# Two-layer hybrid decoder in FP32: operands of the down projection made ahead, their buffers and PSUM banks changed, modulation columns three per step

## The chip, the cores and the metric

The kernel runs on one core of a Trainium2 chip, as one program. The metric is the device time of one execution in microseconds (us), lower is better. Five engines work side by side, each in its own order, and wait for each other by semaphores: PE (TensorE, matmuls; the profile shows its weight loads apart as PEld), DVE (VectorE), ACT (ScalarE), POOL (GpSimd) and SP (SyncE, which here only issues loads and stores). Matmuls write PSUM, which is divided into 8 banks of 512 FP32 columns.

## The reference

The input x is 512 tokens of 1024 channels. Each of two layers has a mixer (an S5 state space part and differential attention) and a SwiGLU feed-forward part, with shift, scale and gate vectors made from a conditioning vector c by one matrix product per layer ("modulation"). The change is in the feed-forward part, which computes

```
m    = silu(c) @ mod_w[l] + mod_b[l]        # 6 x 1024 numbers per layer
h2   = x * (1 + scale2) + shift2
a    = silu(h2 @ w_gate[l]) * (h2 @ w_up[l])   # 512 x 2816
y    = a @ w_down[l]                           # 512 x 1024
x    = layer_norm(alpha * x + gate2 * y)
```

All is FP32.

## The kernel before

FP32 accuracy is had from three matmuls in a faster format: every operand is split into a high part, rounded by ACT, and a low part, the difference, made by DVE; `mm3` issues high x high, high x low and low x high. One use of 128 x 128 weights for 512 tokens is 3 matmuls.

**Weights.** `wunit` loads 512 KB (`wraw`, 2 buffers, issued by SP), lets ACT make `whi` and DVE `wlo` (5 buffers each). They run ahead of PE as far as buffers are free.

**Gate and up.** The 2816 hidden channels are 22 blocks of 128, `fi` = 0 to 21. A step `fi` has two weight units and 48 matmuls into a pair of PSUM banks (`gps`). `swiglu` then has ACT make `sg` and DVE `aT`, and hangs two pieces of background work behind it: `build_bg`, a step of building the S5 tables of the next layer (DVE, POOL, ACT, some PE: `kps` products and `qps` transposes), and `mods_bg`, which computes the modulation columns that were loaded in the step before (a load of 512 KB into `mraw`, a multiplication with a sum on DVE) and issues the loads of the next ones. In layer 0 these are 48 columns: 8 of this layer, whose last are the gate vector `G`, and 40 of the next. Their buffers are the five of tag "C", which `gb`, `G` and `ah` use too.

**Down.** The output is made in two halves of 512 channels, n = 0 and 1, each for four blocks of 128 tokens, t = 0 to 3, into four PSUM banks (`dps`). The loop goes over 11 pairs `fp` of hidden blocks: a weight unit, then for both blocks the operand `ah`, its high part by ACT and its low part by DVE, then 12 matmuls for each block (3 for each t). The last pairs (`TAIL`: 2 in layer 0, 4 in layer 1) are held back and run token block by token block, and after each block `resid_half` multiplies by the gate vector (`rtmp`, DVE), adds to x and takes statistics. In n=1 of layer 0 `norm` and the transposes `htp` for the next layer follow. `gate_tile` writes the gate columns to DRAM (`gd`) and loads them back spread over all partitions (`G`), after the last held `ah`, by a copy on POOL that serves as the order.

PSUM has two banks `acc`, one `s5`, one `po` and two tiles `patt` of two banks each. What waits for a tile waits for all of it: if one half of a pair is read by DVE, a matmul into the other half that stands behind it waits for the read.

What each engine runs, and in what order, follows from the order in the code and a scheduler that keeps it free of waits as far as it can see; `queued` ties background work behind what stands before it.

Of the kernel before, what the change touches and what calls it, by code (L numbers as in the profile page):

```python
# [10 lines left out]
F32R = mybir.dt.float32r  # L11
# [51 lines left out]
def trunk_kernel(tc, xT, x, c, pos, modw, modb, wst, s5a, s5bc, s5d, glub, lamv, subw, lng, lnr, out):  # L63
# [3 lines left out]
    with ExitStack() as es:  # L67
# [257 lines left out]
        def new_hT(name, tag="hT"):  # L325
            hi = [u4(tag, [P, 2, T], F32R, name=f"{name}h{i}") for i in range(4)]
            lo = [u4(tag, [P, 2, T], F32R, name=f"{name}l{i}") for i in range(4)]
            return hi, lo
# [565 lines left out]
        def mods_bg(cols, n, ring, skip=()):  # L894

            with queued(marks(), skip):
                while pend:
                    pend.pop(0)()
                for _ in range(n):
                    if cols:  # L900
                        pend.append(mod_load(*cols.pop(0), ring))
# [33 lines left out]
        for l in range(L):  # L935
# [258 lines left out]
            def swiglu(fi, pgu):  # L1194
                sg = t2([P, T], name="sg")
                nc.scalar.activation(sg, pgu[:, 0], AF.Silu)
                tt(aT[fi // 2][:, fi % 2], sg, pgu[:, 1], ALU.mult)
                if fi > 1:
                    build_bg(builds)
                mods_bg(cols, 2, "C")  # L1200
                if 2 <= fi < 6:
                    with queued(marks()):
                        affine(xt[fi - 2], gb)
# [5 lines left out]
                    gate_up(fi, pgus[fi], w2s[fi], sl)  # L1209
            for fi in range(2):  # L1210
                swiglu(fi, pgus[fi])
            for fi in range(2, NF):
                pgu = patt("gps")
                gate_up(fi, pgu, [wunit(wb + 26 + 2 * fi + i) for i in range(2)], slice(0, T))
                swiglu(fi, pgu)
            sts = [sm([P, 2, 6], "bnst", 5) for _ in range(NT)]
            hTn = new_hT("hTn") if l + 1 < L else None
            TAIL = 2 if l + 1 < L else 4
            for n in range(2):
                if n == 0:  # L1220
                    pss = [patt("dps") for _ in range(2)]
                    pss = [pss[t // 2][:, t % 2] for t in range(NT)]
                else:
                    pss = [acc("dps"), acc("dps"), ppo("dps"), ps5("dps")]

                def dn(fi, w, f2, t, ah):
                    mm3(pss[t], (ah[:, 0, tok(t)], ah[:, 1, tok(t)]), rows(w, f2), fi == 0, fi == NF - 1)

                held = []
                for fp in range(NF // 2):  # L1230
                    w = wunit(wb + 70 + 11 * n + fp)
                    for f2 in range(2):
                        fi = 2 * fp + f2
                        last = l + 1 == L and fp >= NF // 2 - TAIL
                        ah = u4("hT" if last else "C", [P, 2, T], F32R, name="ah")
                        cp(ah[:, 0], aT[fp][:, f2])
                        tt(ah[:, 1], aT[fp][:, f2], f(ah[:, 0]), ALU.subtract)
                        if fp < NF // 2 - TAIL:
                            for t in range(NT):
                                dn(fi, w, f2, t, ah)  # L1240
                        else:
                            held.append((fi, w, f2, ah))
                    if n == 0:
                        build_bg(builds)
                        mods_bg(cols, 1, None)
                if n == 1 and l + 1 < L:
                    gb = load_gb(2 * l + 1, f(held[-1][3][:, 0, 0:1]))
                if n == 0:
                    assert not cols and not builds and not pend
                    G2 = gate_tile(l, 1, f(held[-1][3][:, 0, 0:1]))  # L1250
                    abn = mod_ab(l + 1, 0, 2 * l + 1) if l + 1 < L else None
                for t in range(NT):
                    for fi, w, f2, ah in held:
                        dn(fi, w, f2, t, ah)
# [107 lines left out]
```

## Time and profile before

| | |
|---|---|
| runs | 1279.36, 1279.63, 1282.85 us; median 1279.63 |
| profiled execution | 1279.54 us, span of its instructions 1277.8 us |
| PE busy | 1190.9 us, 93% of the span |
| DVE busy | 841.6 us, 66% |
| ACT busy | 478.9 us, 37% |
| POOL busy | 206.4 us, 16% |
| chain that ended last | PE 68%, DVE 18%, DMA 4%, POOL 3%, issue 3%, ACT 3% |
| mean load, `wraw` / `mraw` | 3.7 / 4.8 us to landing (median), 512 KB each |

The shares are means over the whole program. In the timeline a row gives start, length, engine, line, operation, output and inputs, and in brackets the idle time of the engine before it and what ended it. PEclk is TensorE's granted clock as a part of full speed.

### The profile page before, as it was taken

The page shows a single profiled execution, that of the slowest core. Times are in us where ns is not written, and L with a number is a line of the kernel's source. Part 1 is how long each engine was busy: PE and PEld are TensorE (multiplying, and loading weights), DVE is VectorE, ACT ScalarE, POOL GpSimd, SP SyncE. Part 2 cuts the span into 40 slices and gives each one's busy share as a digit, 9 for nine tenths or more (in the row PEclk, how much of TensorE's full clock was granted, in tenths as well). Part 3 has the DMA queues.
Part 4 walks back from the last instruction along what each step waited for, and adds up shares of the span by engine and source line. Part 5 has one row for each costly group of instructions (what it writes and reads, how often), then busy time and mean ns, then how long its engine had stood idle before and what let it go on. Part 6 is the DMA issues. An engine that isn't in the chain of part 4 may idle for free.

```text
span 1277.8 us, 17430 instructions
## 1 busy us (share of the span) xinstructions
PE 1190.9 (93%) x6608; PEld 992.1 (78%) x6608; DVE 841.6 (66%) x1537; ACT 478.9 (37%) x846; POOL 206.4 (16%) x286
## 2 busy tenths in 40 slices
PE   4768888999999999989899999999999999999997
PEld 3557777688888888867687798878888888888885
DVE  6679999866687576698647557785666222235556
ACT  3413446527322222243346245661733222234330
POOL 8943320001002121132001131100000000000001
PEclk8887999999999999999899999999999999999999
DMA  9654236534665666744333554423463333333241
GB/s 357 226 153 143 65 82 226 158 107 152 195 221 186 226 200 193 252 141 146 117 99 101 186 168 107 131 83 99 151 196 103 98 96 100 99 99 115 66 133 66
DMA packets 66868, 186.57 MB, mean 146 GB/s; under 512 B 7936, under 2 KB 21536, under 8 KB 66784
## 3 DMA queue, kind: packets, MB, share of 16 engines
q1 hardware_dynamic: 62352, 174.88, 43.4%
q0 software_dynamic: 2848, 8.70, 2.1%
q10 hardware_dynamic: 1584, 1.88, 0.5%
q8 instruction: 52, 0.85, 0.3%
q14 instruction: 32, 0.26, 0.1%
HBM read 171.85 MB, written 11.49 MB: 143 GB/s over the span
## 4 chain that ended last, share of the span: by engine, by line
PE 68%; DVE 18%; DMA 4%; POOL 3%; issue 3%; ACT 3%; SPq 0%; DVEq 0%; POOLq 0%; ACTq 0%
PE gps L116 37%; PE dps L116 14%; PE ops L116 4%; PE vps L116 3%; DVE mraw L110 3%; PE ups L116 2%; PE qkps L116 2%; DVE wlo L104 2%; DVE stmp L104 1%; POOL s5tmp L104 1%; DMA mraw<-in_modw 1%; DMA wraw<-in_wst 1%; DVE Gt L104 1%; PE yps L116 1%; PE glups L116 1%
## 5 line engine op out<-in xcount | busy, mean ns | idle before, releaser
L104 DVE TENSOR_TENSOR wlo<-wraw,whi 128x1024 fp32r<-128x1024 f32 x180 | 225.3, 1254 | 266.3 <-ACT whi L113 264.4
L113 ACT ACTIVATE whi<-wraw 128x1024 fp32r<-128x1024 f32 x184 | 194.2, 1058 | 376.6 <-PE gps L116 273.0
L116 PE MATMUL gps<-hT2h,whi 128*128 128x512 f32 (+1 forms) x768 | 286.4, 373 | 0.2
L116 PE MATMUL gps<-hT2l,whi 128*128 128x512 f32 (+1 forms) x768 | 285.7, 372 | 0.0
L116 PE MATMUL gps<-hT2h,wlo 128*128 128x512 f32 (+1 forms) x768 | 285.3, 372 | 0.0
L116 PE MATMUL dps<-whi,ah 128*128 128x512 f32 x704 | 223.7, 397 | 8.2 <-DVE rtmp L104 4.5
L116 PEld LDWEIGHTS gps<-hT2h,whi 128*128 128x128 f32 x768 | 144.6, 188 | 25.8 <-DVE rtmp L104 0.6
L116 PEld LDWEIGHTS dps<-whi,ah 128*128 128x128 f32 x704 | 133.9, 190 | 39.5 <-DVE rtmp L104 6.0
L116 PEld LDWEIGHTS gps<-hT2h,wlo 128*128 128x128 f32 x768 | 144.7, 188 | 25.1
L116 PEld LDWEIGHTS gps<-hT2l,whi 128*128 128x128 f32 x768 | 144.7, 188 | 24.9
L116 PE MATMUL dps<-wlo,ah 128*128 128x512 f32 x352 | 138.5, 393 | 0.0
L110 DVE SCALAR_TENSOR_TENSOR mraw<-mraw,scb 128x1024 f32<-128x1024 f32 x96 | 122.0, 1299 | 1.8 <-DMA mraw<-in_modw 1.6
L113 ACT ACTIVATE ah<-aT 128x512 fp32r<-128x512 f32 x88 | 53.8, 627 | 115.5 <-PE dps L116 93.2
L104 DVE TENSOR_TENSOR ah<-aT,ah 128x512 fp32r<-128x512 f32 x88 | 61.1, 706 | 40.0 <-ACT ah L113 39.6
L116 PEld LDWEIGHTS dps<-wlo,ah 128*128 128x128 f32 x352 | 67.2, 191 | 13.6
L116 PE MATMUL qkps<-whi,hTh 128*128 128x256 f32 x128 | 39.7, 312 | 7.3 <-ACT whi L113 6.5
L116 PE MATMUL ops<-whi,am 128*128 128x512 f32 x128 | 43.4, 398 | 0.0
L116 PE MATMUL qkps<-wlo,hTh 128*128 128x256 f32 x128 | 40.0, 313 | 0.5 <-DVE wlo L104 0.5
L104 POOL TENSOR_TENSOR rs<-rs,mhalf 128x1 f32<-128x1 f32 x16 | 10.8, 676 | 176.8 <-DVE rs L101 176.8
L116 PE MATMUL qkps<-whi,hTl 128*128 128x256 f32 x128 | 39.1, 306 | 0.0
L751 ACT ACTIVATE e<-sps,nm 128x128 f32<-128x128 f32 (+3 forms) x64 | 33.1, 525 | 14.9 <-DVE nm L749 12.8
L116 PE MATMUL qkps<-whi,hTnh 128*128 128x256 f32 x128 | 37.4, 292 | 0.0
(290 smaller groups left out, 1939.4 us busy)
## 6 DMA issues: line engine op xcount, KB each, us to landing
wraw<-in_wst SPq DMA_DIRECT2D x184, 512.0 KB, 3.7
mraw<-in_modw SPq DMA_DIRECT2D x96, 512.0 KB, 4.8
M<-kd SPq DMA_DIRECT2D x64, 64.0 KB, 3.6
gb<-in_lnr SPq DMA_DIRECT2D x8, 512.0 KB, 4.1
xT<-in_xT SPq DMA_DIRECT2D x8, 256.0 KB, 7.1
u<-us SPq DMA_DIRECT2D x32, 64.0 KB, 2.5
csl<-sC SPq DMA_DIRECT2D x8, 256.0 KB, 2.8
x<-in_x SPq DMA_DIRECT2D x4, 512.0 KB, 4.1
```

Of the source, the lines that this page charges most:

```text
L104: (eng or nc.vector).tensor_tensor(out, a, b, op=op)
L110: nc.vector.scalar_tensor_tensor(out, a, s, b, op0=ALU.mult, op1=ALU.mult, accum_out=acc_out)
L113: nc.scalar.activation(out, in_, AF.Copy, scale=scale)
L116: nc.tensor.matmul(ps, a, b, start=start, stop=stop)
L751: nc.scalar.activation(e[:, m, :n], ps[:, m, :n], AF.Exp, bias=nm[:, m : m + 1], accum_out=ss[:, i, m : m + 1])
```

## The change

Four things are changed, and both layers run the same code.

1. Modulation columns: two per step for `fi` under 3, then three.
2. The weights and `ah` of pair (n, fp) = (0, 0) are made ahead of gate and up step 21, those of (0, 1) behind its matmuls, and those of (1, 0) ahead of the token blocks of n = 0 (`operands`, kept in `ready`).
3. In layer 0 the `ah` of n = 0 use the eight "hT" buffers instead of "C", but for the ones made ahead; `hTn`, which also needs "hT", is allocated only after the loop of n = 1.
4. PSUM banks: n = 0 uses `acc`, `acc` and one pair (t = 2, 3); n = 1 uses a pair (t = 0, 1), `po` and `s5`. Before, n = 0 used two pairs, and n = 1 `acc`, `acc`, `po`, `s5`.

```diff
-                mods_bg(cols, 2, "C")
+                mods_bg(cols, 2 if fi < 3 else 3, "C")
...
+            ready = {}
+
+            def operands(n, fp, tag):
+
+                w, ahs = wunit(wb + 70 + 11 * n + fp), []
+                for f2 in range(2):
+                    ah = u4(tag, [P, 2, T], F32R, name="ah")
+                    cp(ah[:, 0], aT[fp][:, f2])
+                    tt(ah[:, 1], aT[fp][:, f2], f(ah[:, 0]), ALU.subtract)
+                    ahs.append(ah)
+                ready[n, fp] = w, ahs
+
             for fi in range(2, NF):
+                if fi == NF - 1:
+                    operands(0, 0, "C")
                 pgu = patt("gps")
                 gate_up(fi, pgu, [wunit(wb + 26 + 2 * fi + i) for i in range(2)], slice(0, T))
+                if fi == NF - 1:
+                    operands(0, 1, "C")
                 swiglu(fi, pgu)
             sts = [sm([P, 2, 6], "bnst", 5) for _ in range(NT)]
-            hTn = new_hT("hTn") if l + 1 < L else None
+            hTn = None
             TAIL = 2 if l + 1 < L else 4
             for n in range(2):
-                if n == 0:
-                    pss = [patt("dps") for _ in range(2)]
-                    pss = [pss[t // 2][:, t % 2] for t in range(NT)]
-                else:
-                    pss = [acc("dps"), acc("dps"), ppo("dps"), ps5("dps")]
+                pair = patt("dps")
+                pair = [pair[:, 0], pair[:, 1]]
+                pss = [acc("dps"), acc("dps"), *pair] if n == 0 else [*pair, ppo("dps"), ps5("dps")]
...
                 for fp in range(NF // 2):
-                    w = wunit(wb + 70 + 11 * n + fp)
-                    for f2 in range(2):
+                    if (n, fp) not in ready:
+                        own = fp >= NF // 2 - TAIL if l + 1 == L else n == 0
+                        operands(n, fp, "hT" if own else "C")
+                    w, ahs = ready.pop((n, fp))
+                    for f2, ah in enumerate(ahs):
                         fi = 2 * fp + f2
-                        last = l + 1 == L and fp >= NF // 2 - TAIL
-                        ah = u4("hT" if last else "C", [P, 2, T], F32R, name="ah")
-                        cp(ah[:, 0], aT[fp][:, f2])
-                        tt(ah[:, 1], aT[fp][:, f2], f(ah[:, 0]), ALU.subtract)
...
                     abn = mod_ab(l + 1, 0, 2 * l + 1) if l + 1 < L else None
+                    operands(1, 0, "C")
+                elif l + 1 < L:
+                    hTn = new_hT("hTn")
                 for t in range(NT):
                     for fi, w, f2, ah in held:
                         dn(fi, w, f2, t, ah)
```

On DVE, where gate and up of layer 0 ends and the down projection begins, this stood before: two columns (`mraw`), then weights and the first `ah`, then `aT` of step 21 and further columns.

```order
L110 SCALAR_TENSOR_TENSOR mraw_4693,mods_116<-mraw_4693,scb_100 128x1024
L110 SCALAR_TENSOR_TENSOR mraw_4695,mods_116<-mraw_4695,scb_100 128x1024
L104 TENSOR_TENSOR wlo_5054<-wraw_5050,whi_5052 128x1024
L104 TENSOR_TENSOR mods_116<-mods_116,mbt_102 128x8
L104 TENSOR_TENSOR ah_4900<-aT_2938,ah_4900 128x512
L104 TENSOR_TENSOR wlo_5095<-wraw_5091,whi_5093 128x1024
L104 TENSOR_TENSOR aT_2948<-sg_4849,gps_4788 128x512
L107 SCALAR_TENSOR_TENSOR ksb_4869<-mask16_88,s5dt_114,ksb_4869 128x16
L110 SCALAR_TENSOR_TENSOR mraw_4784,mods_116<-mraw_4784,scb_100 128x1024
L110 SCALAR_TENSOR_TENSOR mraw_4786,mods_116<-mraw_4786,scb_100 128x1024
L104 TENSOR_TENSOR ah_4915<-aT_2938,ah_4915 128x512
L104 TENSOR_TENSOR QT_4930<-pw_3572,s5bc_4689 128x512
```

The first `ah` stands four rows behind the first of these columns. In the changed order the same place reads so; `ah_4996` belongs to pair fp = 2, and the `ah` of pairs 0 and 1 stand 30 to 40 rows further up.

```order
L104 TENSOR_TENSOR Gt_4800<-Gt_4800,ta_4805 128x4x128
L104 TENSOR_TENSOR wlo_5052<-wraw_5048,whi_5050 128x1024
L104 TENSOR_TENSOR ah_4996<-aT_2940,ah_4996 128x512
L104 TENSOR_TENSOR ah_4999<-aT_2940,ah_4999 128x512
L104 TENSOR_TENSOR ah_5054<-aT_2941,ah_5054 128x512
L104 TENSOR_TENSOR ah_5057<-aT_2941,ah_5057 128x512
L104 TENSOR_TENSOR ah_5092<-aT_2942,ah_5092 128x512
L104 TENSOR_TENSOR ah_5095<-aT_2942,ah_5095 128x512
L104 TENSOR_TENSOR wlo_5090<-wraw_5086,whi_5088 128x1024
L104 TENSOR_TENSOR aT_2948<-sg_4894,gps_4821 128x512
L107 SCALAR_TENSOR_TENSOR ksb_4914<-mask16_88,s5dt_114,ksb_4914 128x16
L104 TENSOR_TENSOR QT_4950<-pw_3580,s5bc_4723 128x512
```

No column is left here, and `ah` of pairs 2 to 4 come ahead of `aT` of step 21.

On PE, at the start of the down projection of layer 0, before: `dps_4892` holds t = 0 and 1, `dps_4893` t = 2 and 3, and both names stand for a pair of banks.

```order
L470 MATMUL kps_4852<-s5bc_4689 32x16 x8
L116 MATMUL dps_4892<-whi_4896,ah_4900 128x512
L116 MATMUL dps_4892<-wlo_4898,ah_4900 128x512
L116 MATMUL dps_4892<-whi_4896,ah_4900 128x512 x2
L116 MATMUL dps_4892<-wlo_4898,ah_4900 128x512
L116 MATMUL dps_4892<-whi_4896,ah_4900 128x512
L116 MATMUL dps_4893<-whi_4896,ah_4900 128x512
L116 MATMUL dps_4893<-wlo_4898,ah_4900 128x512
```

After: `dps_4924` and `dps_4925` are single banks for t = 0 and 1, `dps_4923` is the pair for t = 2 and 3, and `whi_4811` and `ah_4815` are those made ahead.

```order
L470 MATMUL kps_4897<-s5bc_4723 32x16 x8
L116 MATMUL dps_4924<-whi_4811,ah_4815 128x512
L116 MATMUL dps_4924<-wlo_4813,ah_4815 128x512
L116 MATMUL dps_4924<-whi_4811,ah_4815 128x512
L116 MATMUL dps_4925<-whi_4811,ah_4815 128x512
L116 MATMUL dps_4925<-wlo_4813,ah_4815 128x512
L116 MATMUL dps_4925<-whi_4811,ah_4815 128x512
L116 MATMUL dps_4923<-whi_4811,ah_4815 128x512
```

The matmuls stand in nearly the same order, on other banks and with operands made earlier.

On PE, at the end of n = 0 of layer 0, before: the end of block t = 2 and, from the fourth row on, the start of t = 3 (both `dps_4893`).

```order
L116 MATMUL dps_4893<-whi_5367,ah_5374 128x512
L116 MATMUL dps_4893<-wlo_5369,ah_5374 128x512
L116 MATMUL dps_4893<-whi_5367,ah_5374 128x512
L116 MATMUL dps_4893<-whi_5355,ah_5359 128x512
L116 MATMUL dps_4893<-wlo_5357,ah_5359 128x512
L116 MATMUL dps_4893<-whi_5355,ah_5359 128x512
```

After: the end of t = 2 and, from the fifth row on, the start of t = 3 (both `dps_4923`), with four matmuls of n = 1 between them (`dps_5455`, the pair for its t = 0 and 1; the last of the three rows counts twice).

```order
L116 MATMUL dps_4923<-whi_5360,ah_5367 128x512
L116 MATMUL dps_5455<-whi_5381,ah_5385 128x512
L116 MATMUL dps_5455<-wlo_5383,ah_5385 128x512
L116 MATMUL dps_5455<-whi_5381,ah_5385 128x512 x2
L116 MATMUL dps_4923<-whi_5348,ah_5352 128x512
L116 MATMUL dps_4923<-wlo_5350,ah_5352 128x512
```

Before, t = 3 follows t = 2 at once, while five matmuls of t = 2 stand between t = 0 and t = 1; in the changed order this sharing of a pair is left for t = 2 and 3 alone, and matmuls of n = 1, whose first operands are ready, stand between.

## Rows read from the trace of the kernel before

**Rows 1.** Table by stretches, layer 0 (busy us of each engine).

```profile
core 0: us, PE busy (x) PEld busy (x) DVE busy (x) ACT busy (x) POOL busy (x), PEclk, DMA share, GB/s
349.00:399.00 50.00, 50.00 (x222) 41.42 (x221) 38.80 (x93) 11.69 (x15) 7.03 (x8) 1.00 0.70 221
499.00:535.00 36.00, 36.00 (x164) 29.81 (x163) 18.74 (x29) 9.97 (x14) 3.04 (x5) 1.00 0.75 243
...
550.00:570.00 20.00, 19.46 (x81) 15.27 (x82) 20.00 (x38) 9.29 (x16) 2.35 (x4) 0.91 0.35 101
```

**Rows 2.** PE timeline, down projection of layer 0 to block t=3.

```profile
545.39 0.59 PE L470 MATMUL kps<-Gt,s5bc 128*32 128x112 f32 x16
545.79 0.29 PE L470 MATMUL kps<-s5bc 128*32 128x16 f32 x16
548.01 0.50 PE L116 MATMUL dps<-whi,ah 128*128 128x512 f32 x1 [1.93 <-ACT ah L113]
...
550.23 1.04 PE L116 MATMUL dps<-whi,ah 128*128 128x512 f32 x2 [1.49 <-DVE ah L104]
...
561.15 0.73 PE L116 MATMUL dps<-whi,ah 128*128 128x512 f32 x2 [0.31 <-DVE ah L104]
...
604.67 0.65 PE L489 MATMUL qps<-ident,QT 128*128 128x128 f32 x4 [1.03 <-ACT Q L113]
605.09 0.47 PE L116 MATMUL dps<-whi,ah 128*128 128x512 f32 x1
...
612.79 0.80 PE L116 MATMUL dps<-whi,ah 128*128 128x512 f32 x1 [3.55 <-DVE rtmp L104]
...
621.11 0.50 PE L116 MATMUL dps<-whi,ah 128*128 128x512 f32 x1 [0.96 <-DVE rtmp L104]
```

**Rows 3.** The table by stretches, two short stretches of half n=0.

```profile
549.00:552.00 3.00, 1.77 (x5) 1.00 (x5) 3.00 (x7) 0.56 (x2) 0.00 (x0) 0.75 0.47 139
613.00:616.00 3.00, 3.00 (x8) 2.32 (x9) 1.15 (x2) 0.00 (x0) 0.00 (x0) 0.50 0.26 108
```

**Rows 4.** PE timeline, two matmuls of half n=1.

```profile
676.55 0.39 PE L116 MATMUL dps<-wlo,ah 128*128 128x512 f32 x1
...
680.63 0.39 PE L116 MATMUL dps<-wlo,ah 128*128 128x512 f32 x1
```

**Rows 5.** Tile dps in layer 1: ns min/median/max, first and last start.

```profile
L116 PE MATMUL dps<-whi,ah x352: 388/389/500, 1148.8 to 1268.9; 128*128 128x512 f32 x176
```

**Rows 6.** Timeline of DVE and POOL where the down projection begins.

```profile
543.94 3.35 DVE L110 SCALAR_TENSOR_TENSOR mraw<-mraw,scb 128x1024 f32<-128x1024 f32 x1
...
544.02 1.12 POOL L104 TENSOR_TENSOR QT<-pw,s5bc 128x512 f32<-128x512 f32 x1
```

**Rows 7.** Tile mraw on DVE: ns min/median/max, first and last start.

```profile
L110 DVE SCALAR_TENSOR_TENSOR mraw<-mraw,scb x10: 1212/1217/3352, 542.8 to 586.0; 128x1024 f32<-128x1024 f32 x10
```

**Rows 8.** Groups by line, gate and up of layer 0.

```profile
L110 DVE SCALAR_TENSOR_TENSOR mraw<-mraw,scb 128x1024 f32<-128x1024 f32 x40 | 54.8, 1407 | 0.0
L113 ACT ACTIVATE whi<-wraw 128x1024 fp32r<-128x1024 f32 x45 | 47.7, 1061 | 162.3 <-PE gps L116 126.6 <-DMA wraw<-in_wst 34.4 <-DVE wlo L104 1.3
```

**Rows 9.** Timeline around the load of G.

```profile
604.62 0.58 POOL L520 DMA_DIRECT2D sC<-cs  x1 [6.12 <-ACT Q L113]
...
607.29 0.58 SPq L313 DMA_DIRECT2D G<-gd  x1
...
612.04 0.69 DVE L104 TENSOR_TENSOR rtmp<-dps,G 128x512 f32<-128x512 f32 x1 [2.44 <-DMA G<-gd]
```

**Rows 10.** DMA issues from 299 to 590 us.

```profile
s5bc<-in_s5bc ACTq DMA_DIRECT2D x4, 128.0 KB, 3.6
```

**Rows 11.** Timeline, end of layer 0: POOL and PE.

```profile
681.86 0.55 POOL L104 TENSOR_TENSOR rs<-rs,mhalf 128x1 f32<-128x1 f32 x1 [2.76 <-DVE rs L101]
...
683.21 0.18 POOL L332 COPY gb<-ah 128x1 f32<-128x1 f32 x1 [0.50 <-PE dps L116]
...
686.02 0.76 PE L850 MATMUL htp<-ident,x 128*128 128x128 f32 x5 [1.25 <-ACT ht L856]
```

## The prediction

> **What bounds the kernel now.** I began with the table by stretches. While the gate and up projections of layer 0 run, TensorE (PE) is busy all the time, 50.00 of 50 in the stretch from 349 us, and VectorE (DVE) has room: 38.80 of 50. When the down projection begins this turns round: DVE is busy 20.00 of 20 us and PE falls behind [rows 1]. Then I took every idle PE stretch of the down projection of layer 0 from the timeline, which names what ended each. There are six: 1.93 us for ScalarE's (ACT) `ah`, 1.49 and 0.31 for DVE's `ah`, 1.03 for `Q`, 3.55 and 0.96 for DVE's `rtmp` [rows 2]. They add up to 9.27 us, and they cost more than they last, since the granted clock falls behind them: 0.75 in 549 to 552, and 0.50 (the lower of the two levels) in 613 to 616, where 8 matmuls are done in 3 us [rows 3]. At the full clock one takes 0.2267: from 676.55 to 680.63 PE starts 18 [rows 4].
>
> So what can be won is counted from the top. The last `kps` ends at 545.79 + 0.29 = 546.1, and the block of tokens t=3 of half n=0 starts at 621.11: 75.0 us [rows 2]. The work in between is 252 matmuls (22 x 4 x 3 less the 12 of t=3) at 0.2267, which is 57.1; four groups of `qps` transposes at 605.09 - 604.67 = 0.42, which is 1.7; and one more pair of `kps` groups at 0.7 (545.39 to 546.1). Sum 59.5. **Lost: 15.5 us.** In layer 1 nothing of the kind is in the trace: its 528 matmuls run from 1148.8 to 1268.9, which is 0.228 for each [rows 5], so the change has nothing to win there.
>
> **The change, part by part.**
>
> *Operands made ahead.* The first wait stands because DVE makes the `ah` of fi=0 only after two modulation columns and a `wlo`; the second column started at 543.94 and took 3.35 us [rows 6]. In the new order both `ah` of fp=0, their weights and those of fp=1 stand on DVE before the end of gate and up, and the first 48 matmuls (10.9 us) wait for nothing that is made after it. This removes the rows at 548.01, 550.23 and 561.15 with their clock loss. The four copies and four subtractions are the same work as before, only earlier; they lie beside PE's 50.00 of 50 as long as DVE keeps up (below). The weights of fp=0 now pass ahead of those of the last gate and up step in SP's loads and in the ring of five buffers, so that step has one unit less of lead; the `ah` hold four of the five "C" buffers, which no column needs by then; and `hTn` takes its "hT" buffers after n=0 has given them back. I cost all three at nothing.
>
> *Columns three per step.* Ten columns run on DVE from 542.8 to 587.2 [rows 7], at least 12.1 us of the stretch in which DVE is full. With three per step from the fourth step on, 6 + 14 x 3 = 48 are done by fi=16, and none is left in the down projection. The price is paid under gate and up: a step of 48 matmuls lasts 10.9 us; DVE spends 38.80/50 of it, 8.5 us, and one more column at the mean of 1.41 [rows 8] makes 9.9. That fits. The loads: two weight units and three columns of 512 KB make 2.62 MB a step, 241 GB/s for 193 before. The DMA engines moved 221 GB/s at a share of 0.70 and 243 at 0.75 [rows 1], about 320 when full, so a step's loads need some 8.2 us of 10.9, and the S5 builds' small traffic still fits. The weights also have a lead: ACT's `whi` waits 126.6 us for PE to give back a buffer and only 34.4 for a load [rows 8], so up to four units of 5.4 us lie ready, and a step that runs over by one or two us shows nowhere. Cost taken: 0, bounds 0 to 2.
>
> A row speaks against this: the column of 3.35 us ran while POOL multiplied `QT` from 544.02 on, 2.13 longer than the usual 1.22 [rows 6, 7]. If all of POOL's work held DVE up one for one, a step would grow by 7.03/50 of 10.9, which is 1.5: 9.9 + 1.5 = 11.4, half a us too much, 7 us over 14 steps. That is less than the lead, so even this bound costs PE nothing. The Trainium skill (SBUF — State Buffer, "Who interferes with whom") has a rule for this: a DVE instruction with two SBUF inputs contends with a GpSimd instruction that reads SBUF, and the one that comes second blocks for the whole instruction. The row at 543.94 agrees with it (3.35 beside POOL's work on `QT`), and by it each further column would be exposed in the same way; the sum by it is the bound just given, against 9.9 by the mean.
>
> *PSUM banks.* Before, all of n=0 lies in two pair tiles, so the tail blocks t=1 and t=3 each wait until `rtmp` has read the neighbour: the waits of 3.55 and 0.96 [rows 2]. Now t=0 and t=1 have banks of their own, and only t=3 waits, for `rtmp` of t=2, with four matmuls of n=1 put in between. `rtmp` takes 0.69 [rows 9]; with some 0.4 to be released and to release, less 4 x 0.2267 = 0.9, that leaves 0.2. The 3.55 was longer because `rtmp` waited 2.44 for `G`, whose load was issued at 607.29, behind POOL's `sC` at 604.62, and let it start at 612.04 [rows 9]. With the DVE backlog gone the S5 builds end earlier, and the columns that `G` is made of are long done. I place the landing of `G` near 593 (a hand count along the new order, an estimate) for a need at 601. In n=1 the sharing is new: t=1 waits for `rtmp` of t=0, again behind four matmuls, in both layers: 0.2 each, bounds 0 to 1.
>
> *What stays.* The first `qps` come after 48 matmuls, at 546.1 + 10.9 = 557.0. DVE's `QT` for them stands behind a scaling of `s5bc`, whose load by ACT takes 3.6 to land [rows 10]; I place it at 551, three operations of up to 0.69 and a POOL collision of 2 to 3 us take it to 555 to 556. That is just in time. The second `qps` needs ACT's `Q` of the first, which lost 1.03 before [rows 2]. I take 1.0 for both, bounds 0 to 2.5.
>
> *The end of the layer.* The order on POOL changes: both `gb` copies now stand ahead of the `rs` of t=1, and the second waits for PE until 683.21 while that `rs` ran at 681.86. So `rs` comes up to 683.21 + 0.18 - 681.86 = 1.5 later, and PE already waits 1.25 for `ht` there [rows 11]. I take half, 0.7, bounds 0 to 1.5 and a little more for what follows.
>
> *Sum.* 15.5 - 1.0 - 0.2 = 14.3 in n=0; less 0.4 for n=1 of both layers, less 0.7 at the end: 13.2 us. The profiled execution took 1279.54 (span 1277.8 and 1.7 around it), 0.1 below the median of 1279.63, so 1279.54 - 13.2 gives **1266.3**. With the bounds (stalls that stay 0.5 to 4.5 in all) 1264.5 to 1268.7.
>
> **The rivals.**
>
> *Part of the waits only moves (1269 to 1275).* PE takes its instructions in order, so a late `QT` stops it with all of n=0 behind. For it: DVE and POOL share this work, the margin is 1 to 2 us by an estimate, and one collision costs 2.13 [rows 6, 7]. One such miss of 3 us with a fall of the clock behind it (1.5, by the half of some 3 us) costs 4.5: 1270.8. If `G` is again last in its queue, the 3.55 stays with the half clock behind it, together near 6: 1272. Against: ten columns less on DVE, and a margin of 8 us for `G`.
>
> *The gate and up stage starves (slower than before).* SP issues all loads in order, and a third column that waits for a free buffer holds back the weights behind it. It decides when a step's loads or DVE need so much longer than 10.9 us that 14 steps lose the lead (up to 21 us) and the 13.2 won: 34/14 = 2.4 a step, 13.3 us in all. For the loads that would be 197 GB/s at most, and the same engines moved 243 [rows 1]; for DVE it would be 3.4 more than my 9.9. At 14 us a step the time would be 14 x 3.1 - 21 - 13.2 = 9 above 1279.5, near 1289. Little speaks for it but the row of 3.35.
>
> *Nothing changes (1276 to 1283).* The stage could keep its length if the first `QT`, `Q` and `G` together eat all of the 15.5. Against it: 9.27 us of the waits name operations that now stand earlier or use other banks.
>
> *More than forecast (under 1264.5).* All stalls at zero, and the `htp` wait of 1.25 gone with the earlier end of n=1.
>
> **Chances.** Forecast 0.63, waits move in part 0.20, no change 0.07, slower 0.06, more 0.04. Two runs of this kernel are told apart from about 0.3% (3.8 us) on: faster means under 1275.8, slower over 1283.5. Faster takes the forecast, the larger gain and nearly all of the part gain, 0.86; the same 0.08; slower 0.06. The range takes the forecast, most of the larger gain and the lower half of the part gain: 1263.5 to 1272.5, some 0.78.
>
> **What would show it.** Right: the first `dps` follows `kps` without a stop, PE's clock stays 1.00 from 546 to 620, no `mraw` on DVE after about 510, DVE below 17 of 20 us in the first stretches of the down projection, `G` landed before the first `rtmp`, block t=3 near 607. Wrong: idle PE before `gps` ended by DVE `wlo` or ACT `whi` (starved), before `qps` ended by DVE `QT` (moved), or a longer row of `htp` waits at the end of layer 0 (the copies on POOL). Most likely to make me wrong are the two estimated times, of `QT` and of `G`.

## The result, and the profile after

The changed kernel takes **1267.1 us** (median of 4 runs, 1265.94 to 1267.26) against 1279.56 for the kernel before on the same chip: ratio 0.9895, 95% interval 0.9878 to 0.9912. Forecast were 1266.3 and a range of 1263.5 to 1272.5. The profiled execution took 1265.94 us with a span of 1264.2, 13.6 less than before.

The table by stretches of the changed kernel, same columns as [rows 1]:

```profile
349.00:399.00 50.00, 50.00 (x222) 41.39 (x221) 42.63 (x99) 11.71 (x15) 6.72 (x8) 1.00 0.82 259
...
550.00:570.00 20.00, 20.00 (x94) 16.55 (x93) 17.88 (x33) 7.07 (x11) 6.13 (x8) 1.00 0.21 69
...
640.00:700.00 60.00, 57.95 (x266) 46.40 (x265) 42.78 (x87) 31.33 (x55) 5.80 (x11) 1.00 0.38 118
```

DVE has 17.88 of 20 us left to do at the start of the down projection, PE is busy in all of it and at PEclk 1.00, where it had 0.91. Under gate and up DVE went from 38.80 to 42.63 of 50 and the DMA share from 0.70 to 0.82. What PE loses now lies in 640 to 700.

The PE timeline at the start of the down projection, which answers to [rows 2]:

```profile
545.36 0.59 PE L470 MATMUL kps<-Gt,s5bc 128*32 128x112 f32 x16
545.77 0.29 PE L470 MATMUL kps<-s5bc 128*32 128x16 f32 x16
545.99 0.50 PE L116 MATMUL dps<-whi,ah 128*128 128x512 f32 x1
```

The first `dps` starts at once. Up to the end of n=0 no row of PE has an idle time; the six waits are gone. At the start of block t=3, which is the third matmul of the row at 606.48 (the first two belong to n=1):

```profile
606.25 0.39 PE L116 MATMUL dps<-wlo,ah 128*128 128x512 f32 x1
606.48 1.00 PE L116 MATMUL dps<-whi,ah 128*128 128x512 f32 x3
607.31 0.40 PE L116 MATMUL dps<-wlo,ah 128*128 128x512 f32 x1
```

The three matmuls in the row at 606.48 span 0.83 up to the next row, instead of 0.68: 0.15 is all that is left of the wait ahead of t=3 (0.2 was forecast). The first `rtmp` no longer waits for a load [rows 9]; `G` was issued at 587.3 and landed 3.5 later, ten before its use:

```profile
600.84 0.69 DVE L104 TENSOR_TENSOR rtmp<-dps,G 128x512 f32<-128x512 f32 x1 [0.92 <-PE dps L116]
```

And no column is left in the down projection; the 48 run from 326.5 to 507.2 (tile view, columns as [rows 7]):

```profile
L110 DVE SCALAR_TENSOR_TENSOR mraw<-mraw,scb x48: 1161/1219/3404, 326.5 to 507.2; 128x1024 f32<-128x1024 f32 x48
```

To see where the 13.6 us came from I cut each profiled execution at four points of PE: the first `gps` of layer 0, the `kps` group right behind the last `gps` (it ends gate and up), the first `ups` of layer 1 and the first `gps` of layer 1. Lengths of the stretches in us, worked from the starts of those rows in one profiled execution of each kernel, beside the medians of all runs:

| kernel | median | gate and up | down, to first `ups` | to first `gps` of layer 1 |
|---|---|---|---|---|
| before | 1279.6 | 246.9 | 141.15 | 219.2 |
| changed | 1267.1 | 247.5 | 126.08 | 220.7 |
| e1 columns alone | 1270.1 | 249.1 | 128.73 | 220.7 |
| e2 operands alone | 1279.5 | 246.9 | 143.23 | 219.1 |
| e3 banks alone | 1282.4 | 246.9 | 143.38 | 220.5 |
| e4 `gb` behind `rs` | 1266.4 | 250.8 | 126.09 | 220.6 |
| e5 store later, end of n=0 | 1269.4 | 246.8 | 132.42 | 220.6 |
| e6 old banks in n=1 | 1267.0 | 253.9 | 126.16 | 219.2 |
| e7 operands not ahead | 1267.2 | 248.5 | 126.39 | 222.2 |
| e8 two columns | 1274.9 | 246.8 | 136.67 | 220.6 |
| e9 store in n=1 | 1265.8 | 246.9 | 126.06 | 222.2 |
| e10 store in n=1, old banks there | **1264.5** | 246.9 | 126.18 | 219.3 |
| e11 old banks in n=0 and 1 | 1274.5 | 251.5 | 132.38 | 219.1 |
| e12 `ah` in "C" buffers | 1267.3 | 247.8 | 126.96 | 220.7 |

The stretch ahead of the first `gps`, which no edit touches, lasts 295.3 to 300.1 us in these executions. Totals of single executions can thus differ by some us where no edit is, and the stretches are the better witness. In e1, e7 and e9 the last column holds some 1.5 us of a lower clock in layer 1 (see the last section).

So the down projection gave 15.1 us. Two stretches that were counted at 0 and at 0.7 took back 0.6 and 1.5, which leaves 13.0; the other 0.6 of the 13.6 lie ahead of the first `gps` (297.87 for 298.48) and are not the change's. The end of layer 0 with its transposes reads:

```profile
670.57 1.11 PE L850 MATMUL htp<-ident,x 128*128 128x128 f32 x8 [0.92 <-ACT x L844]
...
672.77 0.50 PE L116 MATMUL ups<-whi,hTnl 128*128 128x512 f32 x1 [0.62 <-DVE hTnl L104]
...
675.15 0.50 PE L116 MATMUL ups<-whi,hTnl 128*128 128x512 f32 x1 [0.41 <-DVE hTnl L104]
```

In place of the one wait of 1.25 in [rows 11] there are three. The first of them, like the one of 1.25, ends ahead of the first `ups` (671.44) and so belongs to the middle stretch; the other two, 0.62 and 0.41, are new in the last one and are 1.0 of its 1.5. The other loss is inside gate and up, one wait of PE's `kps` for DVE's table `Gt` of an S5 build, which the kernel before doesn't have:

```profile
478.26 0.59 PE L470 MATMUL kps<-Gt,s5bc 128*32 128x112 f32 x16 [0.54 <-DVE Gt L104]
```

### The profile page after: what moved, and what is told of

It reads as the page before. It is cut to its first block, busy times and chain, and to the rows that moved or that the text cites. A ratio compares the mean times of both kernels' runs of the same rounds, so it can differ in the third digit from the quotient of the medians.

```text
span 1264.2 us, 17428 instructions
## 1 busy us (share of the span) xinstructions
PE 1187.4 (94%) x6608; PEld 991.5 (78%) x6608; DVE 840.4 (66%) x1537; ACT 479.2 (38%) x846; POOL 206.4 (16%) x286
## 4 chain that ended last, share of the span: by engine, by line
PE 73%; DVE 16%; DMA 4%; ACT 3%; issue 3%; POOL 1%; SPq 0%; DVEq 0%; ACTq 0%; POOLq 0%
PE gps L116 36%; PE dps L116 18%; PE ops L116 5%; PE vps L116 3%; DVE mraw L110 2%; PE ups L116 2%; PE qkps L116 2%; DMA wraw<-in_wst 2%; DVE stmp L104 1%; DVE wlo L104 1%; PE yps L116 1%; DVE x L107 1%; DVE S L104 1%; PE po L116 1%; PE glups L116 1%
## 5 line engine op out<-in xcount | busy, mean ns | idle before, releaser
L104 DVE TENSOR_TENSOR wlo<-wraw,whi 128x1024 fp32r<-128x1024 f32 x180 | 221.4, 1233 | 253.5 <-ACT whi L113 251.5
L116 PE MATMUL dps<-whi,ah 128*128 128x512 f32 x704 | 219.6, 391 | 0.0
```

The costliest lines, as they stand in the source:

```text
L104: (eng or nc.vector).tensor_tensor(out, a, b, op=op)
L116: nc.tensor.matmul(ps, a, b, start=start, stop=stop)
```

## The experiments

Two questions stood open: which of the four parts did it, and what took back some 2 us. All ratios are against the kernel before, run on the same chip.

**e1, the columns alone.**

```diff
-                mods_bg(cols, 2, "C")
+                mods_bg(cols, 2 if fi < 3 else 3, "C")
```

> The kernel before with three columns per step from fi=3 on, and nothing else of the change. If the DVE backlog of ten columns is the common cause of the late operands and of the late G (theory A): the first ah comes 1 to 2 us after the end of gate and up instead of 2.6 and 4.8, G lands before the first rtmp, the wait of 3.55 us shrinks to under 1 and the clock does not fall; what stays is the wait for t=3 near 1 us. Time 1268 to 1271. If the shared PSUM banks are a cause of their own (theory B): the wait ahead of t=1 stays over 2 us with the half clock behind it, and the time is 1272 to 1275. Under gate and up PE has no idle time in either.

Measured 1270.09 us, ratio 0.9931 (0.9912 to 0.9951). One number of the change makes 9.5 of its 12.5 us. There is no wait at the start, and in n=0 two short ones stay:

```profile
603.26 0.69 DVE L104 TENSOR_TENSOR rtmp<-dps,G 128x512 f32<-128x512 f32 x1 [2.03 <-DMA G<-gd]
...
604.01 0.50 PE L116 MATMUL dps<-whi,ah 128*128 128x512 f32 x1 [0.81 <-DVE rtmp L104]
...
609.85 0.50 PE L116 MATMUL dps<-whi,ah 128*128 128x512 f32 x1 [1.25 <-DVE rtmp L104]
```

The second is the shared banks without a late `G`. Behind the first `G` is still late, against what I expected: the twelve matmuls of t=0 start at 599.07 and end near 602.1, and `G`, issued at 599.23, lands at 603.14. Theory A holds for the start: the operands were late because DVE was busy with columns.

**e2, the operands alone** (made ahead, with the old columns, banks and buffers; of the edit only the three calls are shown).

```diff
+                if fi == NF - 1:
+                    operands(0, 0, "C")
...
+                if fi == NF - 1:
+                    operands(0, 1, "C")
...
+                    operands(1, 0, "C")
```

> The kernel before with the operands of (0,0), (0,1) and (1,0) made ahead, but two columns per step, the old PSUM banks and the old buffers. Theory A: the two waits at the start go (some 5 us with their clock loss), but the ten columns still run on DVE in n=0, G is as late as before, and the waits ahead of t=1 and t=3 stay. Time 1273 to 1277. Theory B says the same of this one. If the start were all that counted, the time would be 1267.

Measured 1279.50, ratio 1.0000 (0.9987 to 1.0012): nothing, and 2.5 to 6.5 us less than both theories gave it. The first matmuls are ready, but the waits reappear right behind them:

```profile
546.39 0.73 PE L116 MATMUL dps<-whi,ah 128*128 128x512 f32 x2 [0.91 <-DVE ah L104]
549.94 0.79 PE L116 MATMUL dps<-whi,ah 128*128 128x512 f32 x1 [2.81 <-DVE aT L104]
...
612.20 0.80 PE L116 MATMUL dps<-whi,ah 128*128 128x512 f32 x1 [5.76 <-DVE rtmp L104]
```

The row at 549.94 is a wait that I had not seen. The second pair of banks of n=0 is the one that step 21 of gate and up has just filled, so t=2 waits until DVE has made `aT` from it, and with operands made ahead PE comes to t=2 before DVE, which has columns, `wlo` and `ah` ahead of it, comes to that `aT`. What the start gains, this and a longer wait for `rtmp`, which waits for `G` as before, take back; the down projection of the profiled execution is even 2.1 us longer.

**e3, the banks alone.**

```diff
-                if n == 0:
-                    pss = [patt("dps") for _ in range(2)]
-                    pss = [pss[t // 2][:, t % 2] for t in range(NT)]
-                else:
-                    pss = [acc("dps"), acc("dps"), ppo("dps"), ps5("dps")]
+                pair = patt("dps")
+                pair = [pair[:, 0], pair[:, 1]]
+                pss = [acc("dps"), acc("dps"), *pair] if n == 0 else [*pair, ppo("dps"), ps5("dps")]
```

> The kernel before with the new PSUM banks only. Theory A: the start loses as before; t=1 no longer waits, but rtmp of t=0 still starts only when G has landed (near 612), so rtmp of t=2 ends near 617 and t=3 waits 1 to 2 us for it; with the clock kept that wins 3 to 5 us: 1275 to 1277. Theory B: the banks take all of the waits at the end of n=0, some 7 us, 1272 to 1273.

Measured 1282.36, ratio 1.0013 (0.9997 to 1.0029): no gain, where theory A gave 3 to 5 us and theory B some 7; both miss. `rtmp` still waits for `G`, and t=3 waits for the third `rtmp`:

```profile
615.14 0.69 DVE L104 TENSOR_TENSOR rtmp<-dps,G 128x512 f32<-128x512 f32 x1 [4.59 <-DMA G<-gd]
...
619.98 0.80 PE L116 MATMUL dps<-whi,ah 128*128 128x512 f32 x1 [4.48 <-DVE rtmp L104]
```

The wait of 3.55 ahead of t=1 turned into one of 4.48 ahead of t=3. A bank that is free earlier is worth nothing while the read of another hangs on a late load.

**e4, `gb` behind `rs`** (changed kernel; the load of `gb` is tied behind the normalisation of t=1).

```diff
-                if n == 1 and l + 1 < L:
-                    gb = load_gb(2 * l + 1, f(held[-1][3][:, 0, 0:1]))
...
+                        if t == 1:
+                            with queued(marks()):
+                                gb = load_gb(2 * l + 1, f(held[-1][3][:, 0, 0:1]))
```

> The changed kernel with the load of gb tied behind the normalisation of block t=1 at the end of layer 0, so that POOL does rs of t=1 before the two gb copies, as the kernel before did. If the copy ahead of rs is what the end of layer 0 lost (1.4 us there), about 0.6 us of it come back for the copy of 0.77 us, and up to 1.4 with what follows: 0.5 to 1.4 us faster than the changed kernel, 1265.7 to 1266.6. If the loss comes from DVE's order (rtmp of t=2 ahead of the statistics of t=1), the time stays at 1267.1.

Measured 1266.36 (1264.81 to 1267.93), ratio 0.9895 (0.9872 to 0.9919). The total can't tell 0.7 us, the stretch can: 220.6 as in the changed kernel, and the same wait of 0.92, though POOL now does `rs` first:

```profile
669.62 0.93 POOL L104 TENSOR_TENSOR rs<-rs,mhalf 128x1 f32<-128x1 f32 x1 [3.85 <-DVE rs L101]
670.51 0.30 POOL L332 COPY gb<-ah 128x1 f32<-128x1 f32 x2
...
672.25 1.11 PE L850 MATMUL htp<-ident,x 128*128 128x128 f32 x8 [0.92 <-ACT x L844]
```

So the place of the copies on POOL, to which the prediction gave 0.7 us, is not what the end of layer 0 lost.

**e6, old banks in n=1** (changed kernel, new banks in n=0 only).

```diff
-                pair = patt("dps")
-                pair = [pair[:, 0], pair[:, 1]]
-                pss = [acc("dps"), acc("dps"), *pair] if n == 0 else [*pair, ppo("dps"), ps5("dps")]
+                if n == 0:
+                    pair = patt("dps")
+                    pair = [pair[:, 0], pair[:, 1]]
+                pss = [acc("dps"), acc("dps"), *(pair if n == 0 else (ppo("dps"), ps5("dps")))]
```

> The changed kernel with the old banks for n=1 (acc, acc, po, s5), the new ones kept for n=0. If the pair shared by t=0 and t=1 of n=1 is what costs 1.4 us at the end of layer 0 (waits of 0.92, 0.62 and 0.41 us on htp and ups), the stretch from the first ups to the first gps of layer 1 is 219.2 us again instead of 220.6, and the time is 1265.5 to 1266.2. If the order of n=0 or the operands made ahead cost it, it stays at 220.6 and 1267.1.

Measured 1267.00, 1262.45 to 1270.41, ratio 0.9890 (0.9870 to 0.9911). The stretch is 219.2 again: the pair shared by t=0 and t=1 of n=1 cost the 1.5 us. The table agrees throughout: of the six kernels with the old banks in n=1, five have 219.1 to 219.3 there and e1, with its lower clock, 220.7; the eight others have 220.5 and more. How it costs is only partly seen. PE shows no wait inside n=1, but POOL's `rs` of t=1, which the normalisation needs, comes later. In the changed kernel it starts 4.92 us behind that of t=0, and here 3.33 (the rows of t=1, first the changed kernel, then this one):

```profile
668.46 0.55 POOL L104 TENSOR_TENSOR rs<-rs,mhalf 128x1 f32<-128x1 f32 x1
```

```profile
673.20 0.55 POOL L104 TENSOR_TENSOR rs<-rs,mhalf 128x1 f32<-128x1 f32 x1 [2.76 <-DVE rs L101]
```

In the changed kernel DVE runs `rtmp` of t=2 (666.74) ahead of the end of the statistics of t=1 (667.33), here behind it. Whether the shared pair costs by the wait that it puts behind `rtmp` or by this order was not separated. The total didn't follow, because the `kps` wait in gate and up has grown, in a part of the program that this edit doesn't touch:

```profile
481.79 0.98 PE L470 MATMUL kps<-Gt,s5bc 128*32 128x112 f32 x16 [4.24 <-DVE Gt L104]
```

and the clock at its lower level behind it (table by stretches, columns as [rows 1]):

```profile
484.00:487.00 3.00, 3.00 (x9) 2.33 (x8) 3.00 (x3) 0.00 (x0) 2.92 (x2) 0.50 0.84 265
```

That wait is 0.54 to 4.24 us in the profiled runs of the seven kernels with three columns and the store where the change leaves it, and they have gate and up between 247.5 and 253.9 long.

**What delays `Gt`.** In the changed kernel POOL stores the gate columns of layer 1 to DRAM as soon as they are computed, and with three columns a step that is 44 us earlier than before (498.56). POOL's row, and the next row of ACT that waits:

```profile
454.56 0.90 POOL L310 DMA_DIRECT2D gd<-mods  x1 [2.71 <-DVE mods L104]
...
467.76 1.06 ACT L113 ACTIVATE whi<-wraw 128x1024 fp32r<-128x1024 f32 x1 [10.39 <-DMA wraw<-in_wst]
```

The DMA issues of 455 to 470 in the changed kernel (columns as [rows 10]), and of 453 to 468 in the kernel before, near the same place in the program:

```profile
mraw<-in_modw SPq DMA_DIRECT2D x3, 512.0 KB, 11.1
wraw<-in_wst SPq DMA_DIRECT2D x2, 512.0 KB, 11.8
...
s5bc<-in_s5bc ACTq DMA_DIRECT2D x1, 128.0 KB, 12.0
gd<-mods POOLq DMA_DIRECT2D x1, 4.0 KB, 12.4
```

```profile
mraw<-in_modw SPq DMA_DIRECT2D x3, 512.0 KB, 4.9
wraw<-in_wst SPq DMA_DIRECT2D x3, 512.0 KB, 4.3
```

While the store runs (4 KB, which the code lays out as 1024 pieces of 4 bytes), the loads issued beside it take 11 to 12 us. The lead of the weights goes, `whi` waits 10.39 us for its load, DVE's `wlo` and then the build's `Gt` stand behind it, and PE's `kps` behind that. The Trainium skill (DMA: Bandwidth & Descriptors, "Specifications") asks for at least 512 bytes a transfer for the full rate. The trace agrees as far as it goes, since these 4 KB take 12.4 us where a load of 512 KB takes 4.3 to 4.9, and it shows the other side: the price is paid by the loads that run beside it. No run stores the columns in larger pieces, so that the pieces are the reason is not shown.

The store is not new, and its place decides. The kernel before holds up its loads in the same way where it stores these columns, at 498.56 (issues of 498 to 513):

```profile
wraw<-in_wst SPq DMA_DIRECT2D x3, 512.0 KB, 8.1
mraw<-in_modw SPq DMA_DIRECT2D x2, 512.0 KB, 9.8
gd<-mods POOLq DMA_DIRECT2D x1, 4.0 KB, 11.1
```

PE doesn't wait there: the next `kps` that needs a `Gt` is at 545.39, 47 us later, while 454.56 lies 24 us ahead of the one at 478.26.

**e5, the store later** (changed kernel; the store of `gd` for layer 1 tied behind the code of the start of n=1; `gate_out` is the store, taken out of `gate_tile`).

```diff
+                    if l + 1 < L:
+                        with queued(marks()):
+                            gds[l + 1, 0] = gate_out(l + 1, 0)
```

> The changed kernel with one DMA moved: the store of the gate columns of layer 1 to DRAM (gd, 1024 pieces of 4 bytes), which POOL issues at 454.6 us as soon as its columns are done, is tied behind the start of n=1 of layer 0. Theory C (this store stops the loads): in the changed kernel the loads issued at 455 to 460 took 11 to 12 us to land, the weights came late and PE waited 0.5 to 2.4 us for a Gt of the S5 build near 477; with the store moved this wait goes, loads there land in 4 to 6 us, and the time falls by 0.5 to 2.5 us, to 1264.6 to 1266.6. Theory D (three columns a step are too many loads, whatever the store): the wait near 477 stays, and the time stays within 1266.5 to 1267.5.

Measured 1269.35 (1268.86 to 1271.94), ratio 0.9920 (0.9903 to 0.9936). Gate and up is 246.8, without the wait: theory C holds. But the time got longer, against what theory C gave, since POOL reached the store already at 583.94, and it held up the loads there:

```profile
wraw<-in_wst SPq DMA_DIRECT2D x2, 512.0 KB, 11.1
...
gd<-mods POOLq DMA_DIRECT2D x1, 4.0 KB, 12.2
```

A load of weights issued at 588.65 landed at 600.19, and ACT's `whi` started at 600.27. DVE's `wlo` of n=1 stands behind it and ahead of the first `rtmp`, and t=3 paid:

```profile
601.36 1.23 DVE L104 TENSOR_TENSOR wlo<-wraw,whi 128x1024 fp32r<-128x1024 f32 x1 [8.66 <-ACT whi L113]
...
607.34 0.79 PE L116 MATMUL dps<-whi,ah 128*128 128x512 f32 x1 [3.50 <-DVE rtmp L104]
```

**e7, operands not ahead** (changed kernel without the three calls).

```diff
-                if fi == NF - 1:
-                    operands(0, 0, "C")
...
-                if fi == NF - 1:
-                    operands(0, 1, "C")
...
-                    operands(1, 0, "C")
```

> The changed kernel without the operands made ahead (the ah and weights of (0,0), (0,1) and (1,0) are made where they are used, as before); columns, buffers and banks as changed. Theory A (the columns on DVE were the cause of the late first ah): no wait at the start, as with the columns alone, and the time is within 0.5 us of the changed kernel, 1266.6 to 1267.6, but for n=1, whose first operands now come behind the tail of n=0, where up to 1 us may be lost. The prediction's view, that making ahead removes the waits, gives 5 us more: 1271 to 1273.

Measured 1267.19, ratio 0.9900 (0.9880 to 0.9919), as theory A gave it, and 126.39 for 126.08 in the down projection: with the columns out of the way the operands made ahead are worth 0.3 us. Its gate and up is longer by the wait of this run:

```profile
479.36 0.59 PE L470 MATMUL kps<-Gt,s5bc 128*32 128x112 f32 x16 [1.52 <-DVE Gt L104]
```

**e8, two columns** (changed kernel).

```diff
-                mods_bg(cols, 2 if fi < 3 else 3, "C")
+                mods_bg(cols, 2, "C")
```

> The changed kernel with two columns per step again (four of the 48 and a backlog of ten fall into n=0 of the down projection). Theory A: nearly all of the gain goes, as DVE is full where the down projection begins: 1275 to 1280, with waits for DVE at the start and for rtmp, held by G, before t=3. If operands and banks together carry their part without the columns (each alone won nothing, but each left the other's waits): 1271 to 1274.

Measured 1274.89, ratio 0.9956 (0.9942 to 0.9971), at the border of the two expectations. Operands, banks and buffers together win 4.5 us in the down projection without the columns, though each of the first two alone won nothing. DVE stays the cause of what is left, for `ah`, `QT` and `Q`; the wait for `rtmp` that theory A named is not there:

```profile
556.90 0.73 PE L116 MATMUL dps<-whi,ah 128*128 128x512 f32 x2 [1.98 <-DVE ah L104]
...
560.77 0.63 PE L489 MATMUL qps<-ident,QT 128*128 128x128 f32 x4 [1.31 <-DVE QT L104]
...
606.35 0.76 PE L489 MATMUL qps<-ident,QT 128*128 128x128 f32 x4 [2.97 <-ACT Q L113]
```

**e9, the store in n=1** (changed kernel; a copy on POOL that needs an operand of fp=3 holds the store back; `gate_out` as in e5).

```diff
+                    if n == 1 and l + 1 < L and fp == 3:
+                        mk = sm([P, 1], "gmk", 1)
+                        after(mk, f(ahs[1][:, 0, 0:1]))
+                        with queued(marks()):
+                            gds[l + 1, 0] = gate_out(l + 1, 0)
```

> The changed kernel with the store of layer 1's gate columns issued by POOL only after an operand of pair fp=3 of n=1 (near 620 us), where only weights are loaded and G has landed. Theory C: no wait near 477 (gate and up of layer 0 lasts 246.8 us, as with the store moved before), and none at the end of n=0 either (126.1 us from its start to the first ups), so the time is 0.5 to 3 us below the changed kernel, 1264.0 to 1266.5. If a store there holds up the weights of n=1, a wait for whi or wlo stands in n=1 instead, and the time is 1267 or more.

Measured 1265.75 (1265.45 to 1266.86), ratio 0.9895 (0.9875 to 0.9915), against the expected 1264.0 to 1266.5. Gate and up is 246.9 and the down projection 126.06: neither waits any more. The loads of weights beside the store take 11.4 us here too, and PE doesn't notice. The total alone would not show the gain, as the ratio is that of the changed kernel, which ran on another chip. In the profiled run 1.5 us go in layer 1, behind a wait that all kernels have, the clock falling to its lower level after it:

```profile
714.40 0.73 PE L116 MATMUL vps<-whi,hTnh 128*128 128x512 f32 x2 [1.63 <-ACT whi L113]
...
716.00:719.00 3.00, 3.00 (x8) 2.35 (x9) 1.85 (x5) 0.60 (x1) 0.72 (x1) 0.53 0.64 186
```

**e10, the store in n=1 and the old banks there.**

> The same with the old banks for n=1 as well. The two savings stand in different stretches and add: 246.8 us for gate and up, 126.1 to the first ups, 219.1 from there to gate and up of layer 1. Time 1262.5 to 1265.0. If the clock or the end of layer 0 takes it back, it is 1265 to 1267.

Its edit is that of e9 and e6 together. Measured **1264.52** (1262.70 to 1264.72), ratio 0.9880 (0.9860 to 0.9901), and the stretches are 246.9, 126.2 and 219.3. The median is 2.6 us below that of the changed kernel, on another chip; the intervals of the two ratios overlap, and it is the stretches that show both savings. The store now stands here:

```profile
620.47 0.92 POOL L312 DMA_DIRECT2D gd<-mods  x1
```

and the loads of 452 to 468 land nearly as before the change:

```profile
mraw<-in_modw SPq DMA_DIRECT2D x5, 512.0 KB, 4.9
wraw<-in_wst SPq DMA_DIRECT2D x3, 512.0 KB, 4.5
```

The wait in layer 1 that e9's clock fell behind is there too, and the clock stays:

```profile
714.19 0.73 PE L116 MATMUL vps<-whi,hTnh 128*128 128x512 f32 x2 [1.63 <-ACT whi L113]
...
716.00:719.00 3.00, 3.00 (x16) 2.18 (x15) 1.69 (x4) 1.20 (x2) 0.72 (x1) 1.00 0.72 192
```

**e11, old banks in n=0 and n=1** (changed kernel; the edit of e3 undone).

> The changed kernel with the old PSUM banks in both halves (two pairs in n=0; acc, acc, po, s5 in n=1). With G early, t=1 and t=3 each wait about 1 us for rtmp as with the columns alone (0.81 and 1.25 us there), some 2 to 2.7 us more from the start of n=0 to the first ups than 126.1; the end of layer 0 is 1.4 us shorter, as in the run with old banks in n=1. Together 0.5 to 1.5 us slower than the changed kernel: 1267.5 to 1269.

Measured 1274.49, ratio 0.9954 (0.9938 to 0.9971), 5.5 us above the upper end of what I expected: 132.38 in the down projection. It is the wait of e2 again, for the pair that step 21 has filled, with six `ah` ahead of `aT` in DVE's order:

```profile
550.16 6.94 DVE L104 TENSOR_TENSOR ah<-aT,ah 128x512 fp32r<-128x512 f32 x6
...
558.90 0.68 PE L116 MATMUL dps<-whi,ah 128*128 128x512 f32 x1 [4.08 <-DVE aT L104]
```

With operands made ahead, the new banks are worth 6.3 us in the down projection; without them banks and "hT" buffers together 2.3 (e1 against e7).

**e12, `ah` of n=0 in the "C" buffers** (changed kernel).

```diff
-                        own = fp >= NF // 2 - TAIL if l + 1 == L else n == 0
+                        own = l + 1 == L and fp >= NF // 2 - TAIL
```

> The changed kernel with the ah of n=0 in the five C buffers, as before, instead of the eight hT. If the three buffers more do work, ah comes late in n=0 and PE waits there: 1268 or more, with waits for ah or for G, whose buffer is a C buffer too. If the change of buffers only makes room and gains nothing by itself, as I think with DVE below 18 of 20 us, the time is that of the changed kernel within 0.5 us, 1266.6 to 1267.6.

Measured 1267.31, ratio 0.9915 (0.9888 to 0.9942), with 126.96 in the down projection. The total is where the second expectation has it, and can't tell 0.9 us; the stretch shows that the buffers are worth that:

```profile
597.35 0.18 POOL L332 COPY G<-ah 128x1 f32<-128x1 f32 x1 [5.31 <-PE dps L116]
...
606.61 0.50 PE L116 MATMUL dps<-whi,ah 128*128 128x512 f32 x1 [0.78 <-DVE rtmp L104]
```

The first row is the copy ahead of the load of `G`. It waits until PE has done with a "C" buffer, so `G` is issued at 597.55, against 587.28 in the changed kernel, and lands at 601.13, after t=0 has ended. The first `ah` of n=1, which wants a "C" buffer too, is made only at 607.67, so no matmuls of n=1 stand ahead of t=3, which waits 0.78 in place of 0.15.

## Why the prediction was right, step by step

*What bounds the kernel.* Right. 15.5 us were counted as lost from the start of the down projection to t=3, and that stretch with the end of n=1 is 15.1 shorter. To t=3 alone it is 61.0 for 75.0, with 0.9 us of n=1 now inside: 14.9 won, against 14.3 forecast. Counting from the top, work at the full clock against the time it took, gave the size; the six waits alone, 9.27, would have given it too small.

*Operands made ahead.* The waits went as told, but the cause was the columns ahead of `ah` on DVE, and the columns part removes it alone (e1). The prediction's own sentence says so, "DVE makes the `ah` of fi=0 only after two modulation columns and a `wlo`", and then it gave the removal to the wrong part. Worth by itself: nothing (e2), beside the other parts 0.3 (e7).

*Columns three per step.* Cost 0 was taken, bounds 0 to 2; measured 0.6 in the profiled run and 0.9 to 7.0 with the same columns and store in the six other kernels, past the bound in four of them; in e6, which has the 7.0, the clock fell behind the wait. DVE's load was near (9.9 us a step; 42.63/50 of 10.9 is 9.3). The step that failed is the one on loads, "a step's loads need some 8.2 us of 10.9", which divides bytes by a rate and leaves out that an earlier column brings an earlier store of `gd`, during which the loads stand still, at a place where DVE has less time to catch up. It is no matter of two or three columns as such: with the store moved, the same columns cost nothing there (246.8 to 246.9 in e5, e9 and e10).

*PSUM banks.* Right for n=0: t=1 waits no more, t=3 0.15 (forecast 0.2). The gain hangs on `G` not being late (e3) and grows with operands made ahead, through a wait for `aT` that I had not named (e2, e11). For n=1 the cost of 0.2 was too small: together with the 0.7 for POOL's copies 0.9 stood for the end of layer 0, and it lost 1.5; by e6 nearly all of that is the bank, and by e4 the copies have no part in it that shows. The sign that was named, more waiting around `htp`, came, for another reason.

*The early `G`.* The place was right (landing near 593 forecast, 590.8 measured), the reason only in part. The prediction gave it to the end of the backlog on DVE. That alone brings the issue from 607.29 to 599.23 and the landing to 603.14, still 1 us late for the first `rtmp` (e1). What brings it to 587.28 is the third part, the "hT" buffers, which leave a "C" buffer free for `G` (e12: 597.55). The prediction costed that part at nothing and gave it no gain; the margin of 8 us for `G` rests on it.

*What stays.* 1.0 was kept for `qps`, and it was 0: `QT` and `Q` were in time. DVE had 17.88 of 20 us to do in the first stretch, where below 17 was named as a sign.

*Sum.* 13.2 forecast, 12.5 in the medians and 13.6 between the two profiled executions. Without the 0.6 ahead of the first `gps` the latter is 13.0. The stalls that stayed were put in the wrong places: forecast were 1.0 for `qps`, 0.2 for t=3, 0.4 for n=1 and 0.7 for the copies, together 2.3, and measured 0, 0.15, and 0.6 and 1.5 elsewhere, together 2.25. That the sums agree is luck. The upper bound given, 1268.7, is 0.2 above what its own stalls of 4.5 make.

*The rivals.* A late `QT` or a late `G` did not come. Starvation under gate and up did, in small: PE waited there for DVE, 0.54 us, not through SP's order but through the store. That rival had the place and the wrong mechanism. POOL holding up DVE, by the rule of the Trainium skill on the shared port (SBUF — State Buffer, "Who interferes with whom"), stayed far inside its bound: no `mraw` row is longer than 3.404, the median is 1.219 and the mean 1.357, which makes 0.4 us a step of three columns against the bound of 1.5. The second half of that rule, that the one that comes second is held up, is not what [rows 6] show, though the prediction says that they agree: `mraw` started at 543.94, ahead of POOL's `QT` at 544.02, and was still the one that took longer.

## What to carry to other kernels

Ask of several parts of a change which one removes the cause and which only remove its effects: here one number in a background loop made three quarters of the gain, and two of the other parts won nothing alone, because each left a wait that another part removes. When background work is moved forward, follow what becomes ready with it. A store of a few KB can hold up the loads beside it for ten microseconds, as the one of 4-byte pieces does here; put it where the work behind the loads has the most lead. A wait that goes from one block to the next shows in a table of stretches even when the total can't tell it.

## What was not expected of the hardware

A store of 4 KB in pieces of 4 bytes takes 11 to 12 us and holds the loads issued beside it at 8 to 13 us, for 4.3 to 4.9 without it. This showed wherever it stood: at 498.56 in the kernel before, where PE didn't wait, at 454.56 in the changed kernel, at 583.94 in e5, and in e9 and e10 near 620, where it cost nothing. Not every load beside it is held: `G`, issued 0.08 us behind the store in e5, landed in 3.7.

The same wait of 1.63 us in layer 1 was followed by a granted clock of 0.53 in one profiled run and of 1.00 in another. What decides it was not found; it is worth 1.5 us and is in e1, e7 and e9 of the table, whose clock fell there too (0.81 in 720 to 729, 0.56 in 719 to 722 and 0.53 in 716 to 719).
